# A hybrid decoder layer: one probability tile for two key blocks, a first piece ordered by kinds of parts, and a recurrent branch in two groups

## The chip, the cores and the metric

The kernel runs on one core of one Trainium2 chip. The metric is the device time of one execution in microseconds (us), as the median of several runs. The core has five engines that run their own instruction queues side by side and wait for each other by semaphores: TensorE (PE in the profile, with PEld for its weight loads), VectorE (DVE), ScalarE (ACT), GpSimd (POOL) and SyncE (SP, which only issues DMAs here). Matmul results land in PSUM, which has eight banks of 128 partitions x 512 float32 numbers; everything else is held in SBUF tiles of 128 partitions.

## What is computed

One layer over 1040 tokens (16 meta tokens, then 1024 of the input), width 1024. The parts that the change touches are the attention and the recurrent branch:

```python
u = rmsnorm(h, g_pre_mix)
z = u @ w_in                                   # q | k | v | xr | yr
# attention: 8 heads of 64, 2 key/value heads, window 128, one sink logit per head
s = einsum(q, keys of this block and the one before) * HD ** -0.5
valid = (diff >= 0) & (diff < WINDOW) & (kpos >= PAD)      # WINDOW = BLOCK = 128
s = where(valid, s, -1e30)
m = maximum(max(s), sink)
p = exp(s - m);  denom = sum(p) + exp(sink - m)
o = einsum(p / denom, values of both blocks)
# recurrent branch, 512 channels
xr = causal_depthwise_conv(xr)                 # 4 taps
r, i = sigmoid(xr @ w_a + b_a), sigmoid(xr @ w_x + b_x)
log_a = -8 * r * softplus(-lambda);  a = exp(log_a)
hr = scan(a, sqrt(-expm1(2 * log_a)) * (i * xr))
rec = gelu(yr) * hr
h = h + rmsnorm(concat(o, rec) @ w_out)
h = h + rmsnorm(relu(rmsnorm(h) @ w_ff1) ** 2 @ w_ff2)
```

With a window of 128 and blocks of 128, a query in row s of its block sees the keys s+1 to 127 of the block before and 0 to s of its own: 128 keys in all.

## The kernel before

**Products in parts.** Every float32 operand is split into a high part (rounded to the type fp32r, which TensorE takes) and a low part (the rest). A product is three matmuls: high x high, high x low, low x high (`mm3`, L121 to L125). `split` (L92) makes the high part by a copy, mostly on ACT, and the low part by a subtraction on DVE; `split_scaled` does it with a factor.

**Order.** A tile scheduler sets the order of each engine's queue from the program, priorities, and its own model of durations; `behind` adds an ordering between two instructions, `lut` keeps the table functions on ACT in program order, and `deferred` lowers the priority of the "fills". SBUF tiles come from pools by tag ("c" has eight buffers, "d" four, "ws" four), PSUM banks from five tags ("acc", "s", "pt", "o" and so on) with two buffers each.

**First stage.** The tokens come in four pieces (`ALL`, L234) of 272 or 256 columns. For each, `norm_rows` (L212) squares and sums rows on ACT, `rstd_of` (L155) forms the inverse root on POOL (a one-column addition, L158, then a power, L164), DVE scales the rows (L217); `transposed` (L250) turns them by TensorE (L257), and splits the result into the tiles `u` (ACT L116, DVE L117). Then `project` (L220) multiplies with four weight blocks of 128 columns: keys, values, and the first blocks of q and x (the loop at L361). `put_k` (L315) writes each key head in three pieces: the high part on ACT into one half of the partitions, the same high part once more on DVE into the other half (L319), and the low part (L320). The two halves are needed because a score is one matmul over 128 partitions: q's high part in one half and its low part in the other, both against the keys' high part; a second matmul adds the keys' low part. The tile `km` holds the keys of the meta tokens in columns 0 to 15, `vm` their values in rows 0 to 15.

**Attention.** There are eight pairs of a column j (one head of each key/value group) and a half (four blocks of 128 queries). `scores` (L445) forms, for each of two heads and four blocks, scores against 256 keys (the block before and its own): a masked reduction on DVE (L482) adds a mask tile, finds the minimum of the negated scores and writes them; ACT takes the exponential with its sum (via L82); DVE takes the reciprocal (L493) and scales (L495). `attend` (L501) transposes the probabilities in tiles of 128x128 (L510, 16 for a pair), splits them (L95, L98) and multiplies them with the values (L521): one matmul serves the queries of a block and of the next with 256 columns. Between the pairs, a fill projects another block of q, x or y (`next_fill`), so that TensorE has work while the softmax of a pair is under way.

**Recurrent branch.** For each of four chunks of 128 channels, `gates` multiplies with the gate weights, `decay` takes exponential and tanh on ACT, `recur` a square root on ACT and a scan on DVE (L665), `rec_out` the GeLU, a product (L671) and a split. Each change of function table on ACT is an `ACT_TABLE_LOAD`. The chunks' decays and scans are done in two groups, but all GeLUs and `rec_out`s come behind both groups.

**Output projection.** `out_mm` multiplies token tiles with the eight row blocks of W_out; blocks 0 to 3 belong to the attention, 4 to 7 to the chunks 0 to 3 of the recurrent branch. For the first four token tiles, blocks 0 to 3 are done ahead of time; blocks 4 to 7 follow. Behind it come the two feed-forward stages, which the change does not touch except that the square root's table, which `load_root` (L170) loads for the last normalisation, is loaded at another place.

Of the kernel before, what the change touches and what calls it, by code (L numbers as in the profile page):

```python
# [16 lines left out]
P = 128  # L17
D = 1024
KC = D // P
T = 1024  # L20
# [17 lines left out]
def hybrid_layer(  # L38
# [42 lines left out]
    def lut(*args, **kwargs):  # L81
# [9 lines left out]
        last_lut[0] = ins.name  # L91

# [22 lines left out]
    def split_scaled(hi, lo, src, scale):  # L115
        nc.scalar.activation(hi, src, AF.Copy, scale=scale)  # L116
        nc.vector.scalar_tensor_tensor(  # L117
            lo, src, scale, f32(hi), op0=ALU.mult, op1=ALU.subtract
        )

    def mm3(dst, lhs, rhs, start, stop):  # L121
# [3 lines left out]
        nc.tensor.matmul(dst, ll, rh, start=False, stop=stop, skip_group_check=True)  # L125
# [29 lines left out]
    def rstd_of(ssq_parts, n=P):  # L155
# [8 lines left out]
        nc.gpsimd.tensor_tensor(rs[:n], ms[:n], half_pow[:n], op=ALU.pow)  # L164
        return rs[:n]

# [3 lines left out]
    def load_root():  # L170
        nc.gpsimd.memset(eps_col, EPS)
        root = small.tile([P, 1], F32, name="root", tag="root")
        lut(root, eps_col, AF.Sqrt)
# [38 lines left out]
    def norm_rows(src, n):  # L212
        xn = slot("d", [P, D])
        ssq = small.tile([P, 1], F32, name="ssq", tag="ssq")
        nc.scalar.activation(xn[:n], src, AF.Square, scale=RMS_SC, accum_out=ssq[:n])
        rs = rstd_of([ssq[:n]], n)
        nc.vector.tensor_scalar(xn[:n], src, rs, None, op0=ALU.mult)  # L217
# [14 lines left out]

    ALL = [(0, 272), (272, 256), (528, 256), (784, 256)]
    REAL2 = [(16, 512), (528, 512)]  # L234

# [5 lines left out]
    nc.vector.tensor_copy(vm.rearrange("p a b -> p (a b)"), zero[:, :256])  # L241
# [8 lines left out]
    def transposed(b, xn):  # L250
        t0, n = ALL[b]
        for kc in range(KC):
# [3 lines left out]
            for s, m in xn:  # L256
                nc.tensor.transpose(  # L257
                    pt[:, o : o + m], s[:m, kc * P : (kc + 1) * P], ident[:m, :m]
                )
                o += m  # L260
            uh, ul = u[kc]
            split_scaled(
                uh[:, t0 : t0 + n], ul[:, t0 : t0 + n], pt[:, :n],
                g_mix_col[:, kc : kc + 1],
            )

# [25 lines left out]
    wk = split_w(rk, "b")  # L292
    wv = split_w(rv, "b")
    transposed(0, xn)
    wq = split_w(rq)
    wx = split_w(rx)
# [7 lines left out]


    khh = [slot("b", [P, T], F32R) for _ in range(2)]
    kl = [slot("b", [P, T], F32R) for _ in range(2)]

    vk = [slot("b", [P, 8, P], F32R) for _ in range(2)]
    HALF = (slice(0, HD), slice(HD, P))  # L310
    vt = slot("c", [P, TT])
    for h in range(2):
        nc.gpsimd.memset(f32(kl[h][HALF[1 - h]]), 0.0)

    def put_k(hh, lo, src):  # L315
        for h in range(2):
            r, o = HALF[h], HALF[1 - h]
            nc.scalar.copy(hh[h][r], src[r])
            nc.vector.tensor_copy(hh[h][o], src[r])  # L319
            nc.vector.tensor_tensor(lo[h][r], src[r], f32(hh[h][r]), op=ALU.subtract)  # L320

    def sink_k(acc, t0, n):
        o = 0
        if t0 == 0:
# [10 lines left out]
    def sink_v(acc, t0, n):  # L335
        nc.scalar.copy(vt[:, t0 : t0 + n], acc)
# [963 lines left out]
```

## Time and profile before

| what | value |
|---|---|
| runs without a profile (3) | 972.04, 972.91, 973.18 us; median 972.91 |
| profiled execution | 974.39 us, of which the span from first to last instruction is 972.6 |
| TensorE clock granted, mean over the span | 0.997 |
| POOL busy in the whole span | 62.5 us, 101 instructions |
| ACT, exponentials of the attention | 64 of 128x257, 0.506 us each, and 0.189 to read the sum |
| DVE, masked reductions | 64, 0.478 us each, and 0.081 to read the result |
| DVE, scalings of probabilities | 64, 0.348 us each |
| TensorE, transposes of probabilities | 128 |
| table loads on ACT | 1.28 us each |

How to read it: the span is one execution as the hardware profiler saw it. An engine's busy share is the time in which it executed anything. TensorE's matmuls are pipelined, so its busy time says that it had work and not that the work went at the highest rate; the distance between the starts of two matmuls is the better price of one. The chain of waits goes back from the last instruction, at each step to what released it. Waits are inferred from semaphores.

### The profile page before, as it was taken

To read this page: it belongs to the slowest core of one execution; us is meant where nothing else is said; L and a number is where in the kernel's file an instruction comes from. 1 tells how busy PE (TensorE), PEld (TensorE's weight loads), DVE (VectorE), ACT (ScalarE), POOL (GpSimd) and SP (SyncE) were. 2 spreads that over 40 slices of the span, in tenths; PEclk is the share of its full clock that TensorE was granted. 3 is DMA by queue.
4 is the path that set the end of the run, shared out by engine and by line. 5 is a ranking of instruction groups with operands and counts; after the bars stand their busy time and mean duration, and the time that the engine had idled before them with its cause. 6 is when DMAs were issued, how large, how long until landed. Compare 5 with 4: busy or idle time off the path is not lost.

```text
span 972.6 us, 12482 instructions
## 1 busy us (share of the span) xinstructions
PE 953.2 (98%) x4782; PEld 801.7 (82%) x4782; DVE 672.6 (69%) x995; ACT 507.5 (52%) x829; POOL 62.5 (6%) x101
## 2 busy tenths in 40 slices
PE   6999999999999999999999999999999999999996
PEld 5999999888778887888788888888888788888885
DVE  6679997774976686665654455468567676779884
ACT  6646673567944554443555556555433343436441
POOL 4100000000002100000000000000111100001201
PEclk9999999999999999999999999999999999999998
DMA  9102101012234566576622263423777766546934
GB/s 275 44 1 66 23 23 44 23 47 69 80 111 151 154 214 202 172 254 187 205 106 87 87 215 112 127 87 110 172 173 193 171 222 200 188 150 184 250 66 87
DMA packets 87931, 129.61 MB, mean 133 GB/s; under 512 B 13592, under 2 KB 52520, under 8 KB 87872
## 3 DMA queue, kind: packets, MB, share of 16 engines
q1 hardware_dynamic: 79504, 106.54, 34.7%
q0 software_dynamic: 7936, 20.97, 10.6%
q10 hardware_dynamic: 432, 1.31, 0.4%
q8 instruction: 37, 0.61, 0.2%
q14 instruction: 22, 0.18, 0.1%
HBM read 109.93 MB, written 18.87 MB: 132 GB/s over the span
## 4 chain that ended last, share of the span: by engine, by line
PE 88%; ACT 3%; DMA 3%; DVE 3%; issue 2%; SPq 0%; DVEq 0%; ACTq 0%; POOLq 0%
PE ps_acc L124 10%; PE ps_acc L123 10%; PE ps_acc L125 10%; PE ps_pt L123 6%; PE ps_pt L125 6%; PE ps_pt L124 6%; PE ps_s L125 6%; PE ps_s L124 6%; PE ps_s L123 6%; PE ps_o L124 5%; PE ps_o L125 5%; PE ps_o L123 5%; PE ps_o L521 2%; DMA d<-in_w_ff_dram 2%; PE ps_pt L510 1%
## 5 line engine op out<-in xcount | busy, mean ns | idle before, releaser
L95 ACT CAST ws<-raw 128x1024 fp32r<-128x1024 f32 (+1 forms) x68 | 69.6, 1024 | 118.3 <-PE ps_o L124 45.2
L98 DVE TENSOR_TENSOR ws<-raw,ws 128x1024 fp32r<-128x1024 f32 (+1 forms) x69 | 82.2, 1192 | 42.6 <-ACT ws L95 42.5
L123 PE MATMUL ps_acc<-a,ws 128*128 128x256 f32 (+2 forms) x272 | 90.5, 333 | 0.6 <-DVE b L320 0.6
L124 PE MATMUL ps_acc<-a,ws 128*128 128x256 f32 (+2 forms) x272 | 89.8, 330 | 0.0
L125 PE MATMUL ps_acc<-a,ws 128*128 128x256 f32 (+2 forms) x272 | 89.4, 329 | 0.0
L95 ACT CAST ws<-e 128x1024 fp32r<-128x1024 f32 x43 | 45.0, 1048 | 65.2 <-PE ps_o L124 42.9
L98 DVE TENSOR_TENSOR b<-b,b 128x1024 fp32r<-128x1024 f32 (+2 forms) x48 | 57.5, 1199 | 26.8 <-PE ps_o L124 18.5
L95 ACT CAST b<-b 128x1024 fp32r<-128x1024 f32 (+2 forms) x48 | 49.3, 1028 | 38.5 <-DVE b L803 36.6
L98 DVE TENSOR_TENSOR ws<-e,ws 128x1024 fp32r<-128x1024 f32 x43 | 52.5, 1221 | 19.2 <-ACT ws L95 19.2
L123 PEld LDWEIGHTS ps_acc<-a,ws 128*128 128x128 f32 x272 | 51.2, 188 | 4.9 <-DVE b L320 0.8
L125 PEld LDWEIGHTS ps_acc<-a,ws 128*128 128x128 f32 x272 | 51.2, 188 | 4.6
L124 PEld LDWEIGHTS ps_acc<-a,ws 128*128 128x128 f32 x272 | 51.2, 188 | 3.9
L124 PE MATMUL ps_acc<-ws,b 128*128 128x512 f32 (+1 forms) x120 | 46.3, 386 | 0.4 <-DVE ws L98 0.4
L125 PE MATMUL ps_acc<-ws,b 128*128 128x512 f32 (+1 forms) x120 | 46.1, 384 | 0.0
L123 PE MATMUL ps_acc<-ws,b 128*128 128x512 f32 (+1 forms) x120 | 46.1, 386 | 0.0
L123 PE MATMUL ps_pt<-ws,b 128*128 128x512 f32 x112 | 44.1, 394 | 0.0
L124 PE MATMUL ps_pt<-ws,b 128*128 128x512 f32 x112 | 44.1, 393 | 0.0
L125 PE MATMUL ps_pt<-ws,b 128*128 128x512 f32 x112 | 44.0, 393 | 0.0
L123 PE MATMUL ps_s<-ws,b 128*128 128x512 f32 x110 | 43.4, 395 | 0.0
L124 PE MATMUL ps_s<-ws,b 128*128 128x512 f32 x110 | 43.3, 393 | 0.0
L125 PE MATMUL ps_s<-ws,b 128*128 128x512 f32 x110 | 43.2, 393 | 0.0
L123 PE MATMUL ps_o<-ws,b 128*128 128x512 f32 (+1 forms) x108 | 41.4, 384 | 0.0
(386 smaller groups left out, 2653.5 us busy)
## 6 DMA issues: line engine op xcount, KB each, us to landing
raw<-in_w_ff_dram SPq DMA_DIRECT2D x61, 512.0 KB, 3.8
e<-in_w_ff_dram SPq DMA_DIRECT2D x45, 512.0 KB, 3.8
d<-in_w_ff_dram SPq DMA_DIRECT2D x12, 512.0 KB, 3.8
s_dram<-d POOLq DMA_DIRECT2D x12, 512.0 KB, 3.9
raw<-in_w_in_dram SPq DMA_DIRECT2D x9, 512.0 KB, 4.0
c<-in_x_dram SPq DMA_DIRECT2D x8, 512.0 KB, 9.1
d<-in_x_dram SPq DMA_DIRECT2D x8, 512.0 KB, 4.9
out_dram<-raw SPq DMA_DIRECT2D x8, 512.0 KB, 2.6
```

What stands on the lines that cost most here:

```text
L95: nc.scalar.copy(hi, src)
L98: low = nc.vector.tensor_tensor(lo, src, f32(hi), op=ALU.subtract).ins
L123: nc.tensor.matmul(dst, lh, rh, start=start, stop=False, skip_group_check=True)
L124: nc.tensor.matmul(dst, lh, rl, start=False, stop=False, skip_group_check=True)
L125: nc.tensor.matmul(dst, ll, rh, start=False, stop=stop, skip_group_check=True)
L510: nc.tensor.transpose(pt[:, o : o + P], sn[h][:, 2 * bp + i, s * P : (s + 1) * P], ident,)
L521: nc.tensor.matmul(po[:, oc : oc + n], v, p_[:, pc : pc + n], start=first and k == 0, stop=last and k == 1, skip_group_check=True,)
```

## The change

**Attention.** `scores` takes one tile for both heads with 128 columns per block instead of 256, and one column for the sink. ACT copies the scores of a query's own block out of PSUM; DVE's predicated copy lays the scores of the block before over them where the key's column lies above the query's row (`above`, a constant tile of ones and zeros). So each query's 128 visible keys share one row of 128. In the first block the columns below 112 are set to a large number (`far`); the meta keys and values move to the last 16 columns and rows of `km` and `vm`. One reduction on DVE finds the minimum over four blocks and the sink; the scaling is one multiplication over 4x128 columns. q is written negated. `attend` transposes four tiles per head instead of eight, splits them, and GpSimd makes of each part two masked copies with `affine_select`: the own-block keys into one half of a tile of [4, 2, 128], the others, in place, in the other half. The products with the values are as before. The sink's column is copied by GpSimd.

**Keys.** The second copy of the high parts is made at the end of the first stage by four DMAs issued by GpSimd from one half of the partitions to the other.

**First piece.** Its matmuls are ordered by kind: for keys and then values all high x high, then weights high x input low; then, for both, weights low x input high. The order of ACT's and DVE's instructions in this piece is fixed by `chained`. The memsets of the keys' low tiles come first in GpSimd's queue. The first transposes of the next pieces are placed behind the matmuls of earlier ones (`after`).

**Recurrent branch.** GeLU, product and split of chunks 0 and 1, and the splits of W_out's blocks 4 and 5, come right behind their scans, ahead of the second group's decays; `out_mm` takes blocks 4 and 5 for the first four token tiles, and then 6 and 7. The table load for the root is put behind the squares of the first feed-forward stage. The fills "x" 3 and "q" 3 change places.

```diff
+    def part(acc, w, piece, k, last=2):
+        t0, n = piece
+        for kc in range(KC):
+            last_mm[0] = nc.tensor.matmul(
+                acc[:, :n], w[k // 2][:, kc, :], u[kc][k % 2][:, t0 : t0 + n],
+                start=k == 0 and kc == 0, stop=k == last and kc == KC - 1,
+                skip_group_check=True,
+            ).ins.name
...
+    khh = [slot("b", [P, T], F32R) for _ in range(2)]
+    kl = [slot("b", [P, T], F32R) for _ in range(2)]
+    HALF = (slice(0, HD), slice(HD, P))
+    for h in range(2):
+        nc.gpsimd.memset(f32(kl[h][HALF[1 - h]]), 0.0)
...
+    def chained(e, ins):
+        if last[e] is not None:
+            behind(last[e], ins)
+        last[e] = ins.name
...
-    wk = split_w(rk, "b")
-    wv = split_w(rv, "b")
+    wk = high_w(rk, "b")
     transposed(0, xn)
-    wq = split_w(rq)
-    wx = split_w(rx)
+    low_w(wk, rk)
+    wv = high_w(rv, "b")
+    low_w(wv, rv)
+    wq = high_w(rq)
+    low_w(wq, rq)
...
+        if b == 0:
+
+            acc = [bank("acc"), bank("acc")]
+            for a, w in zip(acc, (wk, wv)):
+                part(a, w, piece, 0)
+                part(a, w, piece, 1)
+            xn = [(norm_rows(xt[2], P, True), P)]
+            part(acc[0], wk, piece, 2)
+            sink_k(acc[0][:, : piece[1]], *piece)
+            xn.append((norm_rows(xt[3], P, True), P))
+            part(acc[1], wv, piece, 2)
+            sink_v(acc[1][:, : piece[1]], *piece)
+            wx = high_w(rx)
+            low_w(wx, rx)
...
+    for h in range(2):
+        r, o, m = HALF[h], HALF[1 - h], slice(P - NMETA, P)
+        nc.gpsimd.dma_start(f32(khh[h][o]), f32(khh[h][r]))
+        nc.gpsimd.dma_start(f32(km[o, h, m]), f32(km[r, h, m]))
...
-                for i in range(2):
-                    b = 4 * half + 2 * bp + i
-                    k = 2 * bp + i
-                    nc.vector.tensor_tensor_reduce(
-                        out=sn[h][:, k, 0:256], in0=sp_[:, i, :],
-                        in1=mask1 if b == 0 else mask, scale=-1.0,
-                        scalar=nsink[:, j + 4 * h : j + 4 * h + 1],
-                        op0=ALU.add, op1=ALU.min, accum_out=negm[:, h, k : k + 1],
+                s_ = sn[:, h, 2 * bp : 2 * bp + 2, 0:P]
+                nc.scalar.copy(s_, sp_[:, :, P:256])
+                nc.vector.copy_predicated(
+                    s_, above_i.rearrange("p (a b) -> p a b", a=1).to_broadcast([P, 2, P]),
+                    sp_[:, :, 0:P],
+                )
+                if half == 0 and bp == 0:
+                    w = slice(0, P - NMETA)
+                    nc.vector.copy_predicated(sn[:, h, 0, w], above_i[:, w], far)
+            nc.vector.tensor_reduce(
+                negm[:, h, :], sn[:, h], axis=mybir.AxisListType.X, op=ALU.min
+            )
...
+            ph, pl = (slot("c", [P, 4, 2, P], F32R) for _ in range(2))
+            pt = bank("pt")
+            for i in range(4):
+                nc.tensor.transpose(pt[:, i * P : (i + 1) * P], sn[:, h, i, 0:P], ident)
+            pt = pt.rearrange("p (a b) -> p a b", a=4)
+            split(ph[:, :, 0], pl[:, :, 0], pt)
+            for p_ in (ph, pl):
+                for s, g, op in ((1, 1, ALU.is_ge), (0, -1, ALU.is_gt)):
+                    nc.gpsimd.affine_select(
+                        out=p_[:, :, s], in_=f32(p_[:, :, 0]), pattern=[[0, 4], [g, P]],
+                        compare_op=op, fill=0.0, base=0, channel_multiplier=-g,
                     )
...
+        at[0][2 + cs[0] // 2] = pair("b", [P, 2, 512])
+        for c in cs:
+            for half in range(2):
+                y = ys[c][:, 512 * half : 512 * half + 512]
+                lut(y, y, AF.Gelu_apprx_tanh)
+        for c in cs:
+            rec_out(c, 0, nc.vector if c == 1 else None)
+        for kc in range(4 + cs[0], 6 + cs[0]):
+            load_wo(kc, ("d", "raw")[kc % 2])
+            split_wo(kc, "a")
...
+    for t in range(4):
+        out_mm(t, pos[t], range(4, 6))
```

In the order that the scheduler makes of the changed kernel, the masked copies of a pair stand in GpSimd's queue in a row, mixed over the two heads in the first two pairs; TensorE's queue has scores, fills and transposes between a pair's transposes and its products with the values; the gate matmuls come behind the last products of the attention and two fills, where before they were mixed with them. The feed-forward stages have the same order as before on TensorE.

261 lines of the change are left out of this document (142 added, 119 removed).

## The prediction

> **What bounds the kernel now.** I read the page's busy table and chain first, then TensorE by stage, then single stretches. The table and the chain agree on the engine:
>
> ```profile
> span 972.6 us, 12482 instructions
> PE 953.2 (98%) x4782; PEld 801.7 (82%) x4782; DVE 672.6 (69%) x995; ACT 507.5 (52%) x829; POOL 62.5 (6%) x101
> ...
> PE 88%; ACT 3%; DMA 3%; DVE 3%; issue 2%; SPq 0%; DVEq 0%; ACTq 0%; POOLq 0%
> ```
>
> TensorE (PE) is busy 953.2 of 972.6 us and 88% of the chain. So an instruction taken from it counts in full, and work moved between other engines counts nothing until TensorE waits for it. The stretches say where TensorE is idle; the columns are PE, PEld, DVE, ACT and POOL busy, granted clock, DMA share, GB/s:
>
> ```profile
> 0.00:10.00 10.00, 2.80 (x13) 2.11 (x13) 3.96 (x8) 5.62 (x8) 5.86 (x22) 1.00 0.82 228
> 10.00:20.00 10.00, 8.62 (x42) 7.59 (x43) 8.26 (x14) 8.56 (x17) 4.04 (x7) 1.00 1.12 340
> 20.00:30.00 10.00, 9.43 (x79) 9.15 (x77) 9.18 (x22) 7.59 (x20) 2.35 (x4) 1.00 0.74 203
> 50.00:230.00 180.00, 180.00 (x1239) 166.98 (x1238) 146.05 (x372) 105.63 (x259) 1.03 (x1) 1.00 0.12 33
> 260.00:270.00 10.00, 9.46 (x41) 7.35 (x40) 9.13 (x10) 7.32 (x10) 0.00 (x0) 1.00 0.17 52
> 270.00:280.00 10.00, 9.45 (x41) 7.38 (x40) 9.78 (x13) 3.52 (x7) 0.00 (x0) 1.00 0.31 101
> ```
>
> In the attention (50 to 230 us) PE never rests, although DVE is busy 146 of 180 us. Idle time in reach of the change is 9.2 us in the first 30 us and 0.54 + 0.55 us around 267 and 272 us, where the recurrent branch hands over.
>
> **Part 1, one tile of probabilities.** A pair of a column j and a half now transposes 8 tiles of 128x128 in place of 16: 64 fewer. Their price is in the chain, eight in a row:
>
> ```profile
> 83.46 0.90 PE ps_pt L510 x8
> ```
>
> 0.90/8 = 0.11 us each, so 64 x 0.11 = **7.0 us** off a saturated PE. In the built order of the changed kernel all other matmuls are there in the same numbers (the transpose for the meta values grows from 16 to 128 rows at the same 0.11 us). DVE loses 64 masked reductions (0.478 + 0.081 us), 64 scalings (0.348) and 16 of 32 low parts (0.684), 69 us; it gains 32 predicated copies of 256 columns out of PSUM (not in the trace: between the 0.42 us of the 128x256 subtraction out of PSUM and the 0.56 of the old reduction; I take 0.45), 16 reductions and 16 scalings over some 512 columns (0.69 each by the 128x512 row) and 8 short copies (0.2): 38 us. ACT gains 32 copies (0.37) and loses 16 of 32 casts (0.58) and 0.1 us per exponential of half the width: about -4 us. Nothing of this is on the path while DVE has its 34 us of room; without that cover the two copies ahead of each reduction would delay the exponentials by 0.8 us.
>
> GpSimd (POOL), idle here before, gets 64 selects of 128x512, and PE waits for them. The trace has none of that size:
>
> ```profile
> 1.26 0.28 POOL masks.py:199 TENSOR_SCALAR_AFFINE_SELECT ident<-ident 128x128 f32<-128x128 f32 x1
> ...
> 1.66 0.47 POOL L382 TENSOR_SCALAR_AFFINE_SELECT mask<-mask 128x128 f32<-128x128 f32 x1
> ...
> 2.09 0.33 POOL L386 TENSOR_SCALAR_AFFINE_SELECT mask<-mask 128x128 f32<-128x128 f32 x1
> ...
> 2.73 0.19 POOL L393 TENSOR_SCALAR_AFFINE_SELECT mask<-mask 128x16 f32<-128x16 f32 x1
> ```
>
> From 16 to 128 columns the time grows by 0.09, 0.14 or 0.28 us per 112 columns; carried on to 512 columns that is 0.60, 0.79 or 1.43 us. I take the middle row, 0.79: the lowest ran while DVE only cleared a tile, the highest while DVE cast one. To this comes waiting for DVE:
>
> ```profile
> 20.58 1.22 DVE L98 TENSOR_TENSOR ws<-e,ws 128x1024 fp32r<-128x1024 f32 x1
> 20.89 0.99 POOL L158 TENSOR_SCALAR ms<-ssq 128x1 f32<-128x1 f32 x1 [1.01 <-ACT d L215]
> ```
>
> A one-column POOL operation of 0.22 to 0.34 us elsewhere takes 0.99 here and ends as the DVE subtraction of two SBUF tiles does. Some 40 us of DVE work in the 126 us over which the attention now runs are of that kind (splits of weights, convolutions, scalings), so one select in three meets one and waits half of about 1 us: +0.2. A select is worth 1.0 us, bounds 0.6 and 1.7.
>
> What it may cost is in the built order. Counting PE's pitches (0.109 us for 128 columns, 0.118 for 256, 0.125 for 272, 0.23 for 512), the first pair has its transposes end at 0.5 and 2.8 us, and asks for the low part of its second head at 11.4. In between lie ACT's cast (to 3.5), 0.3 us of small copies and 7 selects: they fit if one takes up to 1.08 us. The second pair fits up to 1.13, the third and fourth up to 1.25 to 1.30, the last four up to 1.5 and more (their PE order has more fill). At 1.0 us PE waits for nothing; I put in **0.3 us** for pieces of waits. At 1.3 the waits add to 3 us, at 1.5 to 8, at 1.6 to 10.6, at 2.0 to 24 or more.
>
> **Part 2, the first piece.** PE does the same 96 matmuls, but all products of high parts first. Before, DVE splits both weights ahead of the low parts of the input, and POOL's memsets slow it:
>
> ```profile
> 9.05 1.52 DVE L217 TENSOR_SCALAR d<-c,rs 128x1024 f32<-128x1024 f32 x1 [0.77 <-POOL rs L164]
> 9.08 2.38 POOL L313 MEMSET b<- 64x1024 f32 x2
> ```
>
> The same scaling takes 0.75 us alone. With the memsets first in POOL's queue (the meta rows' rstd behind them moves some 0.8 us, which the first token tile at 8.3 us hides), the second tile is ready at 9.8 in place of 10.6. ACT then has one weight behind it instead of two and ends its eight scaled casts at about 13.5 (before 17.8), DVE its low parts at 14.2 (before 18.3). PE starts its run at 13.5 with everything there. It is still slow then: matmuls of 272 columns come every 0.225 us until 18.0 and every 0.123 from there, though the granted clock reads 1.00; the run that ends it began at 13.73, so I take 4.3 us of steady work, to 17.8. [...] Counting on with waits at K's accumulator (0.3 us) and at the fourth weight, whose cast stands in ACT's queue behind two squares of the next rows (2 x 1.25 us; PE waits 0.5), the second piece's matmuls start at 28.2. Before they start at 32.04 with 16 transposes more behind them (1.7 us). Gain 32.0 - 1.7 - 28.2 = **2.1 us**, bounds 0 (ACT's squares wait for their rows) and 3.6 (fast pitch from 14.6).
>
> The keys' second copies leave DVE (8 x 0.42 us, no gain) for four DMAs on POOL's queue, behind one memset and one power (1 us each, long due). The last key part is out at some 8.6 us of PE work before the scores that read the copies; cast 0.8, issue 1.2 and 3.9 us to landing (rows of 512 KB; these have 256) need 5.9. Without that cover it would cost 3 us. The selects queued behind the DMAs come later.
>
> **Part 3, the recurrent branch.** Before, the last scans are late for the products that wait:
>
> ```profile
> 269.19 2.32 DVE c L665
> 271.51 0.59 DVE d L671
> 272.12 0.63 ACT b L95
> 272.79 0.73 PE ps_pt L123 x2
> ```
>
> Afterwards blocks 4 and 5 of W_out, fed by channels 0 and 1, come first, and 6 and 7 after 48 more matmuls (48 x 0.23 = 11 us). From the last gate matmul PE has 36 us of y projections and products of blocks 0 to 3; the first group needs 16 us of ACT and ends on DVE at some 22, the second at about 40 against 47. Both waits go: **1.1 us**. The price is a table load more on ACT (1.28) inside that cover; the bound the other way is 0.5 us, should the splits of W_out come late behind the scans. The square root's table now loads in the first feed-forward stage, where ACT is half idle.
>
> **Sum.** 972.6 - 7.0 - 2.1 - 1.1 + 0.3 = 962.7 us of span. The profiled execution took 974.4, 1.8 more than its span, and the median of the runs is 1.5 below that: 964.5 with a profile, **963.0 us** as a median.
>
> **Rivals.** (a) The selects are partly late (1.15 to 1.5 us each): 963.0 + 1.5 to 8, say 967. For it: the slow row, and the narrow 1.08. Against: two of three rows.
> (b) POOL becomes the bound and the kernel slower. Place: the products with v, behind the selects in POOL's one queue; price: the waits above; it decides from 1.6 us per select, where 10.6 us of waits eat the 10.2 gained. At 2.0: 963 + 24 = 987. For it: 1.43 by the slowest row and up to 1.2 us behind each DVE instruction. [...]
> (c) The first piece pays nothing, because the pitch stays slow or ACT's queue moves the wait: 965.1.
> (d) The transposes were hidden: DVE, 98% busy from 90 to 100 us, paces the attention, and PE only waits elsewhere: 970. Against it: no idle PE in 180 us, and DVE loses 31 us.
>
> **How the numbers follow.** Forecast 0.57 (its own range 960.5 to 965), (a) 0.18, (b) 0.09, (c) 0.10, (d) 0.04, another slip 0.02. 960 to 970.5 holds nearly all of the forecast, (c), (d) and most of (a), over 8 in 10. A difference under 0.2%, 1.9 us, can't be told from none here. Faster: all but (b) and the slips, 0.88; the same 0.03 (the edge of (a) and (b)); slower 0.09.
>
> **What would show it.** Transposes of probabilities: 64, at 0.11 us. Selects: their mean against 1.0 us, and idle PE ahead of the products with v, released by POOL. First piece: PE's pitch against time, and the second piece's first matmul near 28.2. Recurrent branch: no idle PE between 255 and 270 us. The forecast is wrong if the selects average over 1.3 us or PE has over 2 us idle in the attention.

## The result, and the profile after

| | before | after |
|---|---|---|
| median of 6 runs | 972.92 us (972.04 to 974.37) | 966.35 us (964.85 to 967.29) |
| ratio after/before, 95% interval | | 0.9930 (0.9917 to 0.9943) |
| profiled execution: span | 972.6 us | 965.3 us |

The change gains 6.6 us by the medians; 963.0 us, a gain of 9.9, was forecast. The measured median lies above the forecast's own range (960.5 to 965) and inside the wider one (960 to 970.5). The page of the kernel after, its busy table and the shares of its chain:

```profile
span 965.3 us, 12356 instructions
PE 947.6 (98%) x4718; PEld 795.0 (82%) x4718; DVE 651.6 (68%) x833; ACT 503.2 (52%) x845; POOL 120.5 (12%) x183
...
PE 81%; DVE 8%; ACT 4%; issue 3%; DMA 3%; POOL 1%; SPq 0%; DVEq 0%; ACTq 0%; POOLq 0%
```

TensorE still bounds the kernel. It has 64 instructions fewer; DVE lost 21 us of busy time, ACT 4.3, and POOL gained 58. The stretches of the kernel after (columns as before: PE, PEld, DVE, ACT, POOL busy, clock, DMA share, GB/s):

```profile
0.00:10.00 10.00, 3.16 (x16) 2.69 (x17) 3.65 (x7) 5.73 (x9) 5.98 (x20) 1.00 0.80 237
10.00:20.00 10.00, 10.00 (x58) 9.40 (x57) 7.61 (x12) 6.80 (x15) 1.57 (x2) 1.00 1.09 351
20.00:30.00 10.00, 9.09 (x76) 8.88 (x76) 7.00 (x16) 7.62 (x20) 4.51 (x11) 1.00 0.57 157
50.00:180.00 130.00, 130.00 (x953) 122.61 (x952) 102.55 (x197) 81.98 (x249) 51.45 (x74) 1.00 0.13 34
180.00:190.00 10.00, 9.42 (x52) 7.87 (x51) 9.94 (x11) 2.84 (x4) 6.19 (x6) 1.00 0.17 48
250.00:260.00 10.00, 10.00 (x45) 8.11 (x44) 8.10 (x7) 9.13 (x11) 0.00 (x0) 1.00 0.15 53
260.00:270.00 10.00, 9.79 (x42) 7.34 (x40) 9.91 (x13) 3.41 (x6) 0.00 (x0) 1.00 0.32 107
```

The attention stays full up to 180 us, then 0.58 us are idle where it ends; the recurrent branch has 0.21 us idle in place of 0.54 + 0.55. What TensorE waited for, in the kernel after (total us, times, longest):

```profile
PE ps_s L306 <- DVE d L231: 6.1, 1, 6.1
PE ps_acc L253 <- DVE km L370: 0.9, 1, 0.9
...
PE ps_s L127 <- DVE e L99: 0.7, 1, 0.7
PE ps_acc L125 <- ACT a L1090: 0.7, 1, 0.7
PE ps_o L620 <- POOL c L609: 0.6, 1, 0.6
PE ps_pt L125 <- ACT b L96: 0.2, 1, 0.2
```

Line by line these are the start, K's accumulator in the first piece, two waits at the start of the feed-forward stage (the second of them, for ACT, stands in the kernel before too), the selects, and the recurrent branch. Apart from the start they are short, and they don't show where 3 us of the forecast went. For that I made a ledger. I take each landmark's time in TensorE's row, less the pitches of all matmuls ahead of it (0.109 us for 128 columns, 0.1172 for 256, 0.1245 for 272, 0.157 for 344 and 348, 0.2308 for 512, 0.1 for 16); the rest is what TensorE has lost so far, in waits or by a slower pitch. Two traces of each kernel (the second ones come from the experiments below):

| lost up to, us | before | after | mean difference |
|---|---|---|---|
| first matmul of the second piece | 14.57, 13.88 | 12.77, 12.14 | -1.77 |
| first scores | 14.96, 14.28 | 13.54, 12.90 | -1.40 |
| last product with v | 15.96, 15.28 | 15.19, 14.54 | -0.75 |
| last of the y projections that end there | 16.17, 15.49 | 15.29, 14.65 | -0.86 |
| last transposes of the normed rows | 18.13, 17.44 | 16.29, 15.64 | -1.82 |
| 570 us of pitches ahead of the end | 19.74, 19.07 | 19.29, 18.41 | -0.55 |
| last matmul | 22.11, 19.58 | 21.76, 21.57 | +0.82 |

The pitches themselves add to 942.76 us before and 935.78 after: -6.98, the transposes. The column of differences then tells the story. The first piece gains 1.8, the projections give back 0.4 and the attention 0.65, the recurrent branch gains 1.0, and the feed-forward stages, whose instructions the change leaves as they were, give back 2.6: 1.3 up to the row of 570 us, which lies some 42 us behind the last transposes, and 1.4 later. Where the text below speaks of the first 34 us of the feed-forward stage, it counts from those transposes.

### The profile page after: what moved, and what is told of

Its sections match the earlier page's. It is cut to its first block, busy times and chain, and to the rows that moved or that the text cites. A ratio compares the mean times of both kernels' runs of the same rounds, so it can differ in the third digit from the quotient of the medians.

```text
span 965.3 us, 12356 instructions
## 1 busy us (share of the span) xinstructions
PE 947.6 (98%) x4718; PEld 795.0 (82%) x4718; DVE 651.6 (68%) x833; ACT 503.2 (52%) x845; POOL 120.5 (12%) x183
## 4 chain that ended last, share of the span: by engine, by line
PE 81%; DVE 8%; ACT 4%; issue 3%; DMA 3%; POOL 1%; SPq 0%; DVEq 0%; ACTq 0%; POOLq 0%
PE ps_acc L125 9%; PE ps_acc L127 9%; PE ps_acc L126 9%; PE ps_pt L125 6%; PE ps_pt L127 5%; PE ps_pt L126 5%; PE ps_s L127 5%; PE ps_s L125 5%; PE ps_s L126 5%; PE ps_o L125 5%; PE ps_o L126 5%; PE ps_o L127 5%; ACT c L82 1%; PE ps_acc L253 1%; PE ps_o L620 1%
## 5 line engine op out<-in xcount | busy, mean ns | idle before, releaser
L125 PE MATMUL ps_acc<-a,ws 128*128 128x256 f32 (+2 forms) x256 | 85.8, 335 | 0.1
L126 PE MATMUL ps_acc<-a,ws 128*128 128x256 f32 (+2 forms) x256 | 85.4, 334 | 0.0
L127 PE MATMUL ps_acc<-a,ws 128*128 128x256 f32 (+2 forms) x256 | 84.9, 332 | 0.0
L96 ACT CAST ws<-e 128x1024 fp32r<-128x1024 f32 x41 | 42.9, 1045 | 65.4 <-PE ps_o L126 45.9
L99 DVE TENSOR_TENSOR ws<-e,ws 128x1024 fp32r<-128x1024 f32 x41 | 50.1, 1222 | 19.6 <-ACT ws L96 19.6
L609 POOL TENSOR_SCALAR_AFFINE_SELECT c<-c 128x512 fp32r<-128x512 f32 x64 | 52.6, 837 | 71.8 <-ACT c L96 61.9
L125 PEld LDWEIGHTS ps_acc<-a,ws 128*128 128x128 f32 x256 | 48.2, 188 | 4.6 <-ACT c L396 0.4
L127 PEld LDWEIGHTS ps_acc<-a,ws 128*128 128x128 f32 x256 | 48.2, 188 | 4.3
L126 PEld LDWEIGHTS ps_acc<-a,ws 128*128 128x128 f32 x256 | 48.2, 188 | 4.0
```

What stands on the lines that cost most here:

```text
L96: nc.scalar.copy(hi, src)
L99: low = nc.vector.tensor_tensor(lo, src, f32(hi), op=ALU.subtract).ins
L125: nc.tensor.matmul(dst, lh, rh, start=start, stop=False, skip_group_check=True)
L126: nc.tensor.matmul(dst, lh, rl, start=False, stop=False, skip_group_check=True)
L127: last_mm[0] = nc.tensor.matmul(dst, ll, rh, start=False, stop=stop, skip_group_check=True).ins.name
L609: nc.gpsimd.affine_select(out=p_[:, :, s], in_=f32(p_[:, :, 0]), pattern=[[0, 4], [g, P]], compare_op=op, fill=0.0, base=0, channel_multip ...
```

## The experiments

The medians below are those of five runs each (of e10 six, of e11 four, of e8 one); the kernel before ran beside them, at 972.35, 972.29, 972.76 and 974.59 us in the four sets, so differences are taken within a set.

### The parts alone: e3, e2, e1

**e3, the attention alone.** First piece, keys' copies and recurrent order as before the change: the edits of e2, e5 and e1 together, whose diffs stand with them below.

> The changed attention alone: first piece, keys' second copies on DVE and recurrent order as before the change. 64 transposes fewer are 7.0 us; with 0.3 us of waits for the selects (forecast) 972.9 - 6.7 = 966.2, with the 0.65 us that the trace of the changed kernel shows in the attention 966.6. Theory B (a later stage takes back part): 966.9 to 967.5. If the DVE copies of the keys and the old first piece make DVE late for the attention, more than 967.5. As a check of the sum: this gain and those of the other two parts (as their undoing shows them) should add to the 6.6 us measured.

Measured 966.13 us against 972.35: -6.2, ratio 0.9935 (0.9922 to 0.9949). The single tile of probabilities alone gains nearly as much as the whole change. It does so at the pitch of the kernel before in the feed-forward stage (231.01 ns between two 512-column matmuls, told under e11), which the changed kernel doesn't have. That is one reason why this gain and what the undoing of the other parts costs (1.5 us in e2, nothing in e1) add to more than 6.6. From the first scores to the last product with v TensorE loses 1.02 us, as in the kernel before (1.00 in both traces) and not 1.65 as in the changed kernel: the new attention by itself runs free of waits for POOL.

**e2, the old first piece.** The order of the first piece undone, the transfers of the keys kept:

```diff
-    wk = high_w(rk, "b")
-    transposed(0, xn)
-    low_w(wk, rk)
-    wv = high_w(rv, "b")
-    low_w(wv, rv)
+    wk = split_w(rk, "b")
+    wv = split_w(rv, "b")
+    transposed(0, xn)
...
-            for a, w in zip(acc, (wk, wv)):
-                part(a, w, piece, 0)
-                part(a, w, piece, 1)
...
+        project(wk, [piece], sink_k)
```

> The changed kernel with the order of its first piece undone (products block by block, both weights split ahead of the input, memsets behind the rows); the keys' second copies stay DMAs. By the forecast's step +2.1 us, by the stage in the trace +1.8 us up to the second piece's first matmul: 968.2 to 968.5 us median. Rival: the next stages take part of it back (TensorE waited 0.4 us more between the second piece and the first scores after the change), so +1.4, 967.8. Rival that the first piece pays nothing at the end: 966.4.

Measured 967.26 us, -5.1 against before, so +1.5 against the changed kernel (its ratio 0.9946, 0.9933 to 0.9958, overlaps the other's). The ledger up to the second piece reads 13.41 here. All four traces of the old order (two of the kernel before, e2, e3) have 13.4 to 14.6, on average 14.1; five of the new order with the transfers (two of the changed kernel, e1, e4, e6) have 11.0 to 12.8, on average 11.9. By these means the first piece pays 2.2 us, as forecast; single traces scatter by nearly as much. With the spare transposes counted as lost time, e9, e11 and e12 below read 11.7 to 12.0, but e10, whose pitch turned fast late, reads 14.0 with the new order too.

**e1, the old recurrent order.**

```diff
     for cs in ((0, 1), (2, 3)):
         for c in cs:
             decay(c)
         for c in cs:
             recur(c)
-        if cs[0] == 0:
-            load_wo(0, "raw")
...
+    load_wo(0, "raw")
...
+    for c in range(NLRU):
+        rec_out(c, 0)
...
-    for t in range(4):
-        out_mm(t, pos[t], range(4, 6))
```

> The changed kernel with its third part undone: GeLU, the products with y and the splits of W_out's second half stand behind both groups of channels again, and the out projection takes blocks 0 to 3 and then 4 to 7. Theory A (the 1.2 us that TensorE loses more at the start of the feed-forward stage come from this regrouping: with three parts the first four tiles of rows end close together, and their norms and the loads behind them bunch): the two waits near 260 to 270 us come back, +1.1 us, and the feed-forward stage gives 1.2 us back, so 966.3 us median, unchanged within 0.5. Theory B (the start of the feed-forward stage is paced by DVE and the loads of its weights, and takes back a part of whatever is gained ahead of it): the waits come back, +1.1, and at most half of that is taken off again later, so 967.0 to 967.5 us. Forecast's own step: +1.1, 967.4.

Measured 965.78 us, ratio 0.9933 (0.9921 to 0.9946): the changed kernel's own time. The waits did come back; this kernel's waits have

```profile
PE ps_pt L125 <- ACT a L96: 1.1, 2, 0.7
```

and from the y projections to the last transposes of the normed rows it loses 1.93 us, where the changed kernel loses 1.00 and 0.99. Yet the first 34 us of the feed-forward stage lose as much as in the changed kernel (2.69 against 2.85 and 2.74). So theory A was wrong: the regrouped projection is not what slows that stage. Where the 0.9 us went instead is told under e11.

### Is the third order of the out projection needed? e6

```diff
-    for t in range(4):
-        out_mm(t, pos[t], range(4, 6))
...
-        out_mm(t, po, range(6 if t < 4 else 0, KC))
+        out_mm(t, po, range(4 if t < 4 else 0, KC))
```

> The changed kernel with the recurrent branch still in two groups on ScalarE and DVE, but the out projection's matmuls in the old two parts (blocks 0 to 3, then 4 to 7 of each tile of rows). If the third order of the matmuls is what removes the waits (forecast): TensorE reaches block 6 about 11 us sooner than the second group is ready, and 0.5 to 1.1 us of waits come back near 260 to 270 us. If the two groups on DVE alone suffice: no waits. Theory A (the three parts make the first four tiles of rows end close together, which delays the weights of the feed-forward stage): the loads of that stage are issued 0.4 us sooner against the last transposes and the stage loses 1.0 us less; net 0 against the changed kernel. Theory B: the loss there stays.

Measured 967.95 us, 2.2 slower than the changed kernel in the same set. One wait stands in the place of two:

```profile
PE ps_pt L125 <- ACT b L96: 1.9, 1, 1.9
```

Behind this wait the granted clock falls to 0.5 for 3.4 us (from 262.3 us), which costs some 1.7 us more, an estimate (half of the 3.4). So grouping ACT's and DVE's work without regrouping the matmuls is worse than neither: the second group comes later than in one block, and TensorE gets there sooner. The first 34 us of the feed-forward stage lose 2.12 us, still above the 1.59 of the kernel before, against theory A once more.

### The keys' second copies: e5

```diff
         for hh, lo, src in parts:
             ops[1] += low_k(hh, lo, src)
+            ops[1] += [
+                nc.vector.tensor_copy(hh[h][HALF[1 - h]], src[HALF[h]]).ins
+                for h in range(2)
+            ]
...
-        nc.gpsimd.dma_start(f32(khh[h][o]), f32(khh[h][r]))
-        nc.gpsimd.dma_start(f32(km[o, h, m]), f32(km[r, h, m]))
```

> The changed kernel with the keys' second copies made by DVE again (8 copies of 0.42 us, two behind each piece) instead of four transfers on GpSimd's queue. The forecast gave this part no gain and no loss: within 0.5 us of the changed kernel. Rival: the 0.6 us that TensorE waits for selects near 188 us stands in the three traces that have the transfers (the changed kernel, the one with the old recurrent order, the one with the old first piece) and not in the one that has neither of the new parts, so the transfers shift GpSimd's and DVE's order, and without them the time falls by 0.6. Other rival: the copies make DVE late in the first piece, +0.7 us.

Measured 966.42 us against 965.70 for the changed kernel in the same set, within the error of the two. Underneath, two things of opposite sign changed. In the first piece TensorE waits longer for its accumulator:

```profile
PE ps_acc L253 <- ACT c L400: 1.7, 1, 1.7
```

and the ledger up to the second piece reads 13.68, 1.5 more than the changed kernel's 12.14 in this set. Not all of this is the wait: behind it the granted clock falls to 0.5 for 3.4 us (from 21.7 us), which no trace of the changed kernel shows there. In the attention there is no wait for POOL, and 0.73 us are lost from the first scores to the last product, not 1.64. Both rivals of the expectation were right, and they nearly cancel. By one trace of each kernel in this set, the transfers are worth 1.5 us in the first piece (0.9 against the first trace of the changed kernel), where the forecast gave them nothing, and they cost 0.9 in the attention, where it gave nothing either. Why GpSimd's and DVE's work meets otherwise there was not tried further.

### The price of the selects: e4

```diff
-                for s, g, op in ((1, 1, ALU.is_ge), (0, -1, ALU.is_gt)):
+                for s, g, op in 2 * ((1, 1, ALU.is_ge),) + 2 * ((0, -1, ALU.is_gt),):
```

> The changed kernel with every select on GpSimd done twice (the same values): 128 instead of 64, 0.84 us each, so 1.68 us where one was. The forecast's count of slack in the built order gives 10.6 us of waits at 1.6 us per select and 24 at 2.0, so about 13 us at 1.68: 979 us median, with idle TensorE ahead of the products with v, released by GpSimd, in the first four pairs above all. Rival (the order has more room than counted, since TensorE's other work moves ahead of the products): under 5 us, 971. Rival (doubling also slows DVE through shared access): over 985.

Measured 976.00 us, ratio 1.0038 (1.0025 to 1.0051): slower than the kernel before, and by the ratios 10 us above the changed kernel. Its POOL groups and its waits:

```profile
L609 POOL TENSOR_SCALAR_AFFINE_SELECT c<-c 128x512 fp32r<-128x512 f32 x128 | 99.2, 808 | 36.3 <-ACT c L96 30.3 <-DVE c L99 4.8
```

```profile
PE ps_o L620 <- POOL c L609: 4.7, 6, 2.6
PE ps_acc L125 <- ACT ws L96: 2.4, 1, 2.4
```

Two selects of 0.81 us stand where one stood, 1.62 us in all, for which the forecast's count had 10.6 us of waits for POOL. The point of rival (b) is borne out: at 1.6 us per select the gain is eaten. Its price agrees only in the total, and that by luck. The waits for POOL are 4.7 us, under half of the count. 2.4 more are a wait for weights that ACT split late, for a projection behind the attention, and behind that wait the granted clock falls to 0.5 for 3.4 us (from 232.2 us), some 1.7 us by the same estimate; neither was in the count. The rest shows as no single wait.

### The start of the feed-forward stage: e7, e8, e9, e10

The kernel after and the kernel before once more, for second traces.

> The changed kernel itself once more, on the chip on which its variants run. Theory C (two things differ from one execution to the next whatever the kernel: when TensorE's pitch becomes fast in the first piece, seen at 13.5, 14.2 and 16.3 us in three executions of the same first piece, and how long a 512 KB load at the start of the feed-forward stage takes, seen at 4.4 to 5.9 us): the median lies between 965.5 and 967, and the new trace shows other values of the two than the first. If the two are fixed by the code, the trace shows 16.3 us and 5.4 us again.

> The kernel before, for a second trace. Theory C: the load at the start of the feed-forward stage that took 4.4 us from issue to use takes more this time, up to 5.9 as in the five others, TensorE loses 2.2 to 3.2 us in the first 30 us of that stage instead of 1.5, and the pitch in the first piece turns fast at another time than 18.2 us. Theory D (the changed kernels make that load slower): 4.4 us and 1.5 us again.

e7: 965.70 us, ratio 0.9934 (0.9921 to 0.9946); e8: one run, 972.03 us. Theory C was half right. The pitch of the first piece is chance: it turns fast at 14.6 us in e7 and 17.4 in e8, where the first traces have 16.3 and 18.2. The load is not: 4.44 us from issue to use again before (4.42 in the first trace), 5.50 after (5.39), and 4.89 to 5.86 in the six other traces of kernels with the new attention. Theory D stands: it is the changed program that makes this load slow. The lines, first of the kernel before, then of the kernel after; a load is issued by SP, and DVE waits for it:

```profile
371.71 0.77 SPq L800 DMA_DIRECT2D a<-in_w_ff_dram  x1
...
376.13 0.69 DVE L803 TENSOR_TENSOR a<-raw,a 128x512 f32<-128x512 f32 x1 [4.87 <-DMA raw<-in_w_ff_dram]
```

```profile
363.26 0.88 SPq L902 DMA_DIRECT2D a<-in_w_ff_dram  x1
...
368.65 0.69 DVE L905 TENSOR_TENSOR a<-raw,a 128x512 f32<-128x512 f32 x1 [5.84 <-DMA raw<-in_w_ff_dram]
```

What DVE makes of this load reaches TensorE as the low part of a weight (`e`). The matmul that needs it, before and after; only the second waits:

```profile
380.87 0.50 PE L125 MATMUL ps_s<-b,e 128*128 128x512 f32 x1
```

```profile
373.38 0.50 PE L127 MATMUL ps_s<-b,e 128*128 128x512 f32 x1 [0.73 <-DVE e L99]
```

The DMA queues in the 6 us around the load tell the two apart (queue, packets, MB, share of 16 engines). Before, from 370.3 us, only two queues move anything:

```profile
q0 software_dynamic: 287, 1.04, 60.1%
q1 hardware_dynamic: 863, 0.87, 40.9%
```

After, from 361.5 us, a third has one packet among them:

```profile
q0 software_dynamic: 288, 1.05, 59.8%
q1 hardware_dynamic: 702, 0.70, 33.3%
q8 instruction: 1, 0.02, 1.2%
```

That packet is a fetch of 16 KB of instructions. It takes 1.15 us here, among data packets of 0.05 (q1) and 0.2 us (q0) on average. From the first to the last packet of the stores (q0) it is 5.0 us here and 4.2 before, and the loads (q1) come behind them. That what is queued behind the fetch on its DMA engine comes later is my reading of this; the trace does not name the DMA engine of a packet. Such fetches come every 29 us or so where TensorE works steadily on 512 columns (29.2 us on average behind 340 us), which is the time of some 128 matmuls of 0.23 us with their weight loads, and there are 37 of them for the 4718 matmuls of the kernel, one for every 127.5: by this count I take them for TensorE's own.

With 64 matmuls fewer, the fetches fall half a period from where they fell: 6.3 and 34.3 us behind the last transposes of the normed rows before, 21.9 us after, and 20.7 to 21.5 us in the seven others. The load is issued at 20.4 to 21.0 us on that scale. That is theory E; e9 moves the fetch by a few instructions that TensorE has idle time for:

```diff
+    spare = bank("acc")
+    for _ in range(30):
+        nc.tensor.transpose(spare[:, :16], ident[:16, :], ident[:16, :16])
```

> The changed kernel with 30 more transposes of 16 rows of the identity at the very start, into a PSUM bank that nothing reads; TensorE has no other work there until 6 us. All later instructions stay in their order but for one swap each on DVE and SyncE. Theory E (in all traces with 64 transposes fewer, a 16 KB instruction fetch runs 20.7 to 21.9 us after the last transposes of the normed rows, among the stores and loads at the start of the feed-forward stage, and DVE gets its load 4.9 to 5.9 us after the issue; in both traces of the kernel before the fetches fall 6 us and 34 us after that point and the load takes 4.4): fetches come every 128 matmuls, 29.5 us, so 30 instructions more bring each 30 x 0.23 = 6.9 us forward, to some 14.8 us behind that point, clear of the transfers. The load then takes 4.4 to 4.5 us, TensorE loses 1.5 to 1.7 us in that stretch instead of 2.2 to 2.9, and the median is 964.8 us, some 1 us under the changed kernel. Rival (the fetch is a bystander, the load is slow for another reason): load 5 us or more, loss as before, 966. The 30 transposes may also make the pitch of the first piece fast sooner (up to -0.5 us, ahead of 30 us, seen apart).

> The same with 8 transposes ahead instead of 30. Theory E: the fetch comes only 1.8 us sooner, 19 to 20 us behind the last transposes of the normed rows, still among the stores that the loads queue behind, so the load stays at 4.9 us or more and the median within 0.5 us of the changed kernel. If any transposes ahead help (by waking TensorE's clock, or by chance), this gains as much as 30 do.

e9: 965.09 us (964.52 to 965.22), ratio 0.9916 (0.9903 to 0.9929). e10: 966.45 us, 0.9933 (0.9920 to 0.9947). In e9 the fetch falls 11.9 us behind the transposes (forecast: 14.8), the queues around the load are the two of before, and the load is as fast as before:

```profile
362.13 1.01 SPq L906 DMA_DIRECT2D a<-in_w_ff_dram  x1
...
366.53 0.69 DVE L909 TENSOR_TENSOR a<-raw,a 128x512 f32<-128x512 f32 x1 [4.84 <-DMA raw<-in_w_ff_dram]
```

4.40 us from issue to use, and the stretch loses 1.63 us; before it lost 1.59 and 1.61, after 2.85 and 2.74. In e10 the fetch falls at 19.8 us, ahead of the load's issue but among the stores, the load takes 4.75 (4.9 or more was expected) and the stretch loses 1.97: between the two. e11 and e12 below, whose fetch falls at 11.6 and 12.1 us, have loads of 4.37 and 4.43 us. That the fetch slows the load is shown: 1.2 us of the missing gain is a fetch that the smaller program moved into a load. Why it came 2.9 us sooner in e9 than forecast was not followed up.

### The pitch of the feed-forward stage: e11, e12

The rest of the loss, 1.4 us behind that stretch, has no wait. The mean time from one 512-column matmul to the next over the last 560 us, gaps of 0.26 us and more left out, is 230.97 and 230.95 ns in the two traces before, and 231.75 and 231.76 after: over some 2320 matmuls 1.8 us, of which a few chance gaps in the first trace before hide a part. e5, e6, e9 and e10 have 231.75 to 231.76 too; e1 231.39, e2 231.39, e3 231.01, e4 231.86. Matmul by matmul the times agree between two traces of one program, and of programs that use the buffers alike (r = 0.94 to 0.98), and not between the kernel before, the changed one, e1, e2 and e3 (r = 0.1 and under; e4 lies between, 0.77 to the changed kernel), though all run the same matmuls in the same order there. e11 moves the buffers and nothing else:

```diff
+    zero = slot("ws", [P, 512])
     khh = [slot("b", [P, T], F32R) for _ in range(2)]
...
-    zero = slot("ws", [P, 512])
     nc.vector.memset(zero, 0.0)
```

e12 takes a tile of `raw` there too. Both have the 30 transposes ahead.

> The kernel with 30 transposes ahead, with one line moved: the first tile of the buffers ws is taken ahead of those of b, so that ws lies at 133088 to 149472 bytes of a partition and b above it, in place of b at 133088 and ws at 203808; raw stays on top. Every engine's instructions and their order are the same. Theory F (the mean time from one 512-column matmul to the next in the feed-forward stage is set by where its operands lie: 230.9 ns in both traces of the kernel before, 231.7 in six of the changed kernel's layout, 231.5, 231.5 and 231.0 in three that use the buffers in another order, and matmul by matmul the times repeat between traces of one layout, r 0.94 to 0.98, and not between layouts, r 0.1 at most): the mean changes by 0.2 ns or more, the matmul by matmul agreement with the 30 ahead falls under 0.3, and the time changes with it, 2400 matmuls by the change of the mean, 0.5 us or more, upward or downward. Rival (the mean is set by the program's instructions or by the chip's day): the mean stays at 231.7 within 0.1 and the pattern agrees, r over 0.9.

> As the one above, with raw taken ahead of b too, which is the order of the kernel before: ws, raw, b. Same instructions in the same order. Theory F: again another mean and another pattern; if the distance from ws to b is what counts, the mean is that of the kernel before, 230.9 ns, and the time is some 2 us under that of the 30 ahead, 963 us. If the order in which the slots of b are used counts as well, any value from 230.5 to 232. Rival: 231.7, same pattern.

e11: 966.06 us, ratio 0.9908 (0.9893 to 0.9923). e12: 964.59 us, ratio 0.9899 (0.9884 to 0.9915). They ran on another chip than e9. The mean pitch is 231.45 ns in both, 0.30 ns less than in e9, worth 0.7 us; the agreement with e9 is gone (r = -0.03 and -0.04), and e11 and e12 agree with each other (0.95), though ws and b lie 8192 bytes further apart in e12. This is what theory F expects if places set the pitch. Its stronger form fails: the old order of the buffers does not bring the old 230.97 back; the slots of b are still used in another order, and whether that is the reason was not tried. The chip as such is not what sets the pitch: on one chip e7 has 231.76 and e8 230.95, and across the two chips the patterns of e2 and of e11 and e12 still agree at r = 0.45 and 0.44. But e9's kernel did not run on the second chip, so a part of the chip's in the 0.30 ns is not excluded, and the other 0.5 ns to the kernel before is put down to places without an experiment. What rule makes one place slower than another stays open. The gain of 0.3 ns is smaller than the intervals of the times, so the pitch is shown by the traces, and the time only agrees with it.

This accounts for e1: its slots of b are used in another order than the changed kernel's, its pitch is 0.36 ns lower, 0.8 us over the stage, and that offsets the 0.9 us of waits. The ledger agrees: behind the row of 570 us e1 loses 1.5 us, the changed kernel 2.5 and 3.2.

e12 has the lowest ratio of all: 1.0% under the kernel before in its set, where the changed kernel is 0.7% under in its own, on the other chip.

## Why the prediction was right, and where it was off

**Right: the transposes.** 64 fewer at 0.11 us, 7.0 us; the pitches give 6.98. e3 shows that they were worth it in full, so rival (d) falls.

**Right: the price of a select, and its spread.** Forecast 1.0 us, as 0.79 bare and 0.2 of waiting for DVE. The kernel after (nanoseconds, least, median, most):

```profile
L609 POOL TENSOR_SCALAR_AFFINE_SELECT c<-c x64: 629/635/1650, 86.3 to 187.6; 128x512 fp32r<-128x512 f32 x64
```

Its mean is 0.84: 0.63 bare, for which the lowest of the three rows gave 0.60 and the middle one, which I took, 0.79; and 0.2 of waiting, as forecast. 39 of 64 took the bare time. The other 25 ended with, or behind, a DVE instruction on SBUF tiles; the longest, 1.65 us, began just behind the start of a convolution tap and ended 0.49 us behind the tap's end.

**Right in size, wrong in place: the waits for POOL.** Forecast 0.3 us, and the first two pairs were named as the narrow ones. The 0.58 us stand at the very end of the attention, where the count had room up to 1.5 us and more per select. DVE is the reason. Its queue and POOL's in the kernel after (start, us, then the instruction):

```profile
181.69 1.66 DVE L649 SCALAR_TENSOR_TENSOR b<-d,prm,b 128x1039 f32<-128x1039 f32 x1
...
184.10 0.69 DVE L99 TENSOR_TENSOR c<-ps_pt,c 128x512 fp32r<-128x512 f32 x1
184.71 1.29 DVE L649 SCALAR_TENSOR_TENSOR b<-d,prm,b 128x1038 f32<-128x1038 f32 x1
...
186.97 1.66 DVE L649 SCALAR_TENSOR_TENSOR b<-d,prm,b 128x1037 f32<-128x1037 f32 x1
```

```profile
184.93 4.20 POOL L609 TENSOR_SCALAR_AFFINE_SELECT c<-c 128x512 fp32r<-128x512 f32 x3 [2.67 <-DVE c L99]
```

```profile
189.18 1.25 PE L620 MATMUL ps_o<-c,b 128*128 128x128 f32 x9 [0.58 <-POOL c L609]
```

The low part (184.10) stands behind a tap, POOL waits 2.67 us for it, and then the three selects meet two more taps and take 1.40 each. The taps, 1.29 alone, take 1.66 behind a select: the waiting goes both ways. The slack count charged POOL for DVE, and left DVE's own queue on time. The same shows in DVE's busy time, off the path: it fell by 21 us, where the forecast had 31 without the key copies.

**Right: the first piece, by errors that cancel, which is luck.** Forecast: second piece at 28.2 us; 28.50 and 27.87 in the two traces, 26.8 to 27.7 in six others with the transfers, 29.8 in e10. The pitch turns fast at 16.3 and 14.6 us, not 17.8, which should have brought more; but TensorE loses 1.08 us at K's accumulator in the one trace, and in the other 0.72 there and 0.34 just ahead, for rows that DVE scales, not 0.3. The 0.5 us forecast at the fourth weight did not come. The 4.3 us to the fast pitch were read from a single run. Counted from the first 272-column matmul it takes 2.8 to 3.5 us in eight traces, 5.5 to 6.2 in four, 7.0 and 8.0 in two; all four traces of the old order, with a gap of 0.9 us soon after that matmul, are among the slower six. What sets this time no run shows.

**Right: the recurrent branch.** 1.1 us forecast, 0.96 in the ledger, and e6 shows that the third order of the matmuls is what earns it.

**Wrong: the feed-forward stages, taken as untouched.** This is the step that made the forecast 3.4 us too low. The sum carried every gain through to the end, because the instructions behind the recurrent branch are the same. They are, but their surroundings are not. The fetch of TensorE's instructions moved into a load (1.2 us, shown by e9), and the pitch of the same matmuls is slower by some 1.8 us, shown by the traces. That the buffers lie elsewhere is the likely cause of the second: e11 moved the pitch by 0.7 us that way, and the rest of the 1.8 was not brought back. No rival of the prediction had either. The rest of the gap is small: 0.4 us in the projections, 0.3 in the first piece and 0.3 in the attention. These terms add to 4.0 us, more than the 3.4 that are missing; the gaps in the first trace of the kernel before and the scatter of single traces make up for that.

**Mis-sized with little effect: the keys' transfers.** Forecast to change nothing; the traces of e5 show a gain of 1.5 us in the first piece and a cost of 0.9 in the attention, and the medians 0.7 us, within their error.

**The rivals.** The time lies nearest to that of rival (a), 967, but not for its reason: the selects average 0.84 us and TensorE waits 0.58 us for them. Rival (c) falls with the gain of the first piece. Rival (b) did not come; e4 shows that the point at which it decides was sound, and that its price was right only in the total.

## What to carry to other kernels

When a change takes instructions out of the bounding engine or reorders how buffers are first used, don't take the later stages for a constant (here, by the ledger, they gave back 2.6 us of what was gained ahead of them): look in the trace where that engine's instruction fetches fall against the loads that are on the path, and compare the mean pitch of the same matmuls before and after. In e9, thirty spare instructions in idle time were enough to move a fetch out of the way (from 21.9 to 11.9 us behind the transposes), and in e11 one line moved a layout. A select given to GpSimd took its bare 0.63 us in 39 of 64 cases and up to 1.65 us where it met DVE's work on SBUF tiles, and DVE paid as well (a tap of 1.29 us took 1.66); count the slack of such work with DVE's queue running late.

## What the runs showed of the hardware

- An instruction fetch is one packet of 16 KB; there are 37 for 4718 matmuls in the kernel after, and 37 for 4782 in the kernel before. It took 0.9 to 1.7 us in the first trace before and 0.9 to 1.9 in the first trace after. A load that met one took 4.9 to 5.9 us in eight traces, and 4.4 in five traces without.
- The time from one 512-column matmul to the next runs from 224 to 242 ns with rare exceptions and repeats matmul by matmul between executions of one program (r of 0.94 to 0.96). Its mean differs between programs with the same matmuls (230.95 to 231.86 ns); e11 and e12 point to the places of the operands.
- TensorE's pitch in the first piece turns fast 2.8 to 7.0 us after the first 272-column matmul in ten traces of one order of matmuls. The view reads a granted clock of 1.00 there, but in the first traces of before and after the clock's records begin only where the pitch turns, at 18.14 and 16.28 us, so they don't show the clock ahead of that. A slow matmul costs 0.1 us more (0.227 us for 272 columns in place of 0.125). Between the two traces of the changed kernel, 5.8 and 3.3 us, this goes with 0.6 us of loss up to the second piece.
- Behind three waits of TensorE of 1.7 to 2.4 us the granted clock itself drops to 0.5 for 3.4 us (at 232.2 us in e4, at 21.7 us in e5, at 262.3 us in e6, where the mean from 260 to 270 us is 0.83). Behind the wait of 2.6 us in e4, near 147 us, it stays at 1.00, so the length of the wait alone does not decide.
